# A fused decoder layer on one core: the input norm with its weight spread in PSUM, the first 256 tokens finished ahead

## The chip, the core and the metric

The kernel runs on one core of one Trainium2 chip. Times are device microseconds of a whole execution; the figure that counts is the median of the runs. Profiles come from one profiled execution. The engines are TensorE (PE, with its weight loads PEld), VectorE (DVE, `V` in the code), ScalarE (ACT, `S`), GpSimd (POOL, `G`) and SyncE (SP, `SY`), whose queue issues most loads.

## What is computed

One pre-RMSNorm decoder layer for 512 tokens of width 1024, in float32: norm, one wide input projection, three token mixers side by side (sparse attention, a spatial-gating MLP, an RWKV-7 recurrence), gates, a merge, an output projection, an embedding gate and a final norm. The part that matters here is its beginning:

```
h = x * rsqrt(mean(x*x) + 1e-6) * norm_g
proj = h @ w_in[i]
...
blk = kv[:, idx] + pe[:, None, :]
hid = jax.nn.silu(jnp.einsum('bnlgd,ldh->bngh', blk, w1))
```

The compression branch of the attention takes two 128-column pieces of `proj` (keys and values, kv = 0 and 1) and is the first user of `h`. After it come the RWKV projections (`rs_block`).

## The kernel before

Matrix products run in the rounded type fp32r with a split in two: each operand is a high part (a cast on ACT) and a low part (the difference, on VectorE or POOL), and a product is three matmuls, high by high, high by low, low by high. The normed input is kept transposed as `hH` and `hL` (128 channels x 8 x 512 tokens). `wload` (L66 to L80) does the same for weights: a load of 256 KB on SP's queue into one of four `wr` buffers, the cast L78, the difference L79. `wparts` gathers the pieces; `fm_block` is 24 matmuls of 512 columns for 128 output channels.

The kernel is written with a framework whose planner places the instructions of each engine in an order of its own from a simulated timeline; waits on data and on buffers are put in by it. `tc.issue_after(ins)` makes the instructions in its block that run on the engine of `ins` come after it there.

At the start POOL makes the constants (identity, masks, indicator matrices, L94 to L133), SP loads `x` in four pieces of 128 tokens (L182), and the norm loop (L211 to L226) does for each piece t: the sum of squares on ACT (L214), mean and epsilon on VectorE (L215), the power -1/2 on POOL (L216), the row factor on VectorE over 1024 columns (L217), and then for each half a of the channels four transposes on PE into PSUM (L222), the product with the weight as a per-partition column on VectorE into the buffer `tg` (L224), the cast on ACT into `hH` (L225) and the difference into `hL`, on POOL for a = 0 and on VectorE for a = 1 (L226). The weight column `ngp` comes from a PE transpose of norm_g (L209, L210).

The norm's buffers (pool `xp`) lie on the left side of SBUF; when the pool is closed its place is taken by others, among them `cpp` with `kc2`, `w2t` and `w1t`. The compression weights are loaded, cast and split at L251, held behind a cast of the second 128 tokens on ACT, with the low part on VectorE. Then come the compression products (L252 to L265), in two halves of 256 tokens and for kv = 0 and 1: 24 matmuls of 256 columns each into one of two PSUM buffers `mm_ps`, evicted by four ACT copies into `kc2`. The parameter rows `prow` are loaded by 13 small DMAs (L267), transposed on PE (L269) and copied to `par`, which the RWKV evictions and `blk` (L294) read. `hid` (L301) is the compression's hidden product with `w1t`.

## Time and profile before

| what | value |
|---|---|
| median of 3 runs | 745.41 us (745.38 to 746.82) |
| profiled execution, its own time | 747.35 us |
| its span | 745.6 us |
| PE busy | 716.0 us (96%) |
| VectorE, ACT, POOL busy | 407.6, 354.2, 288.2 us |

The span is what the trace of the core covers; the execution's time has a little around it. An engine's timeline gives for each instruction (or merged group) its start, its duration and, in brackets, how long the engine stood before it and what released it. PE is busy nearly throughout, so its idle stretches are the first thing to look at.

### The profile page before, as it was taken

The numbers are of one execution on the slowest core, as the hardware profiler recorded it, in microseconds if no ns is written. First come the engines' busy times: TensorE is split into PE (matmuls) and PEld (weight loads), VectorE is DVE, ScalarE is ACT, GpSimd is POOL, SyncE is SP. The second block draws the span as 40 slices with busy tenths as digits, with TensorE's granted clock in tenths as the row PEclk, the third lists the DMA queues.
The fourth block names the chain that finished last, engine by engine and source line by source line (L and its number), as shares of the span: only waits on it lengthen the run. The fifth ranks groups of instructions, "written<-read, shape, count | busy, mean of one in ns | idle before, by whom it ended". The sixth has DMA issues, their size and how long they took to land.

```text
span 745.6 us, 13074 instructions
## 1 busy us (share of the span) xinstructions
PE 716.0 (96%) x4941; PEld 606.6 (81%) x4941; DVE 407.6 (55%) x775; ACT 354.2 (48%) x743; POOL 288.2 (39%) x276
## 2 busy tenths in 40 slices
PE   4899999999999999999999999989999999999995
PEld 4788788999878987779877778767877888998995
DVE  6531587758933773645676565397554222226345
ACT  6554555542372332234565554576554333227453
POOL 6444740120220272300144345323445565256563
PEclk9999999999999999999999999999999999999998
DMA  6853122124546364336433212201228333132212
GB/s 200 182 136 100 48 80 71 44 87 140 156 113 215 101 172 124 107 115 203 135 94 105 57 44 70 71 16 42 54 60 267 100 89 124 58 113 72 78 64 114
DMA packets 106689, 78.73 MB, mean 106 GB/s; under 512 B 5569, under 2 KB 97282, under 8 KB 106626
## 3 DMA queue, kind: packets, MB, share of 16 engines
q1 hardware_dynamic: 105890, 75.27, 35.1%
q10 hardware_dynamic: 736, 2.63, 0.9%
q8 instruction: 39, 0.64, 0.4%
q14 instruction: 24, 0.20, 0.1%
HBM read 67.91 MB, written 9.96 MB: 104 GB/s over the span
## 4 chain that ended last, share of the span: by engine, by line
PE 87%; DVE 5%; ACT 2%; issue 2%; DMA 1%; POOL 1%; SPq 1%; ACTq 0%; POOLq 0%; DVEq 0%
PE mm_ps L62 69%; PE s_ps L62 3%; PE o_ps L62 2%; PE g_ps L62 2%; PE p_ps L872 2%; DMA w1t<-in_cmp_w_dram 1%; PE Yp L62 1%; PE r_ps L62 1%; DVE mx L858 1%; PE st_ps L62 1%; PE mx_ps L62 1%; DVE pl L876 1%; PE u_ps L62 1%; PE bk_ps L477 1%; ACT wh L78 1%
## 5 line engine op out<-in xcount | busy, mean ns | idle before, releaser
L79 POOL TENSOR_TENSOR wl<-wr,wh 128x512 fp32r<-128x512 f32 x144 | 192.5, 1345 | 276.5 <-ACT wh L78 255.5
L78 ACT CAST wh<-wr 128x512 fp32r<-128x512 f32 (+1 forms) x194 | 119.4, 620 | 169.6 <-PE mm_ps L62 117.6
L62 PE MATMUL mm_ps<-hH,wh 128*128 128x512 f32 (+1 forms) x440 | 174.2, 396 | 3.8 <-ACT kc L265 2.3
L62 PE MATMUL mm_ps<-hL,wh 128*128 128x512 f32 (+1 forms) x440 | 171.1, 389 | 0.0
L62 PE MATMUL mm_ps<-hH,wl 128*128 128x512 f32 (+1 forms) x440 | 170.7, 388 | 0.4 <-DVE wl L79 0.4
L62 PEld LDWEIGHTS mm_ps<-hH,wh 128*128 128x128 f32 x440 | 82.9, 188 | 21.3 <-ACT kc L265 2.5
L62 PEld LDWEIGHTS mm_ps<-hH,wl 128*128 128x128 f32 x440 | 82.7, 188 | 18.0 <-DVE wl L79 0.6
L62 PEld LDWEIGHTS mm_ps<-hL,wh 128*128 128x128 f32 x440 | 83.0, 189 | 16.5 <-issue 0.2
L62 PE MATMUL mm_ps<-wh,hL 128*128 128x256 f32 (+1 forms) x224 | 64.9, 290 | 0.0
L62 PE MATMUL mm_ps<-wh,hH 128*128 128x256 f32 (+1 forms) x224 | 63.8, 286 | 0.0
L62 PE MATMUL mm_ps<-wl,hH 128*128 128x256 f32 (+1 forms) x224 | 63.6, 285 | 0.0
L79 DVE TENSOR_TENSOR wl<-wr,wh 128x512 fp32r<-128x512 f32 (+1 forms) x50 | 38.0, 769 | 25.2 <-ACT wh L78 25.1
L62 PEld LDWEIGHTS mm_ps<-wh,hL 128*128 128x128 f32 x224 | 42.2, 188 | 1.1 <-issue 0.5
L62 PEld LDWEIGHTS mm_ps<-wh,hH 128*128 128x128 f32 x224 | 42.0, 188 | 1.2 <-issue 0.5
L62 PEld LDWEIGHTS mm_ps<-wl,hH 128*128 128x128 f32 x224 | 42.2, 188 | 0.5
L876 DVE TENSOR_TENSOR pl<-p_ps,ph 128x512 fp32r<-128x512 f32 x40 | 27.2, 685 | 25.9 <-ACT ph L875 25.9
L62 PE MATMUL mm_ps<-ysH,wh 128*128 128x512 f32 x96 | 38.6, 402 | 0.1
L62 PE MATMUL mm_ps<-ysL,wh 128*128 128x512 f32 x96 | 38.4, 400 | 0.2 <-DVE ysL L722 0.2
L62 PE MATMUL mm_ps<-ysH,wl 128*128 128x512 f32 x96 | 38.2, 398 | 0.0
L859 ACT ACTIVATE P<-s_ps,mx 128x512 f32<-128x512 f32 (+3 forms) x64 | 33.4, 532 | 7.9 <-DVE mx L858 5.5
L62 PE MATMUL mm_ps<-wh,mH 128*128 128x256 f32 x128 | 36.1, 286 | 0.6 <-DVE x L921 0.6
L62 PE MATMUL mm_ps<-wl,hT 128*128 128x256 f32 x128 | 35.9, 281 | 0.0
(336 smaller groups left out, 1437.6 us busy)
## 6 DMA issues: line engine op xcount, KB each, us to landing
wr<-in_w_in_dram SPq DMA_DIRECT2D x130, 256.0 KB
wr<-in_w_branch_dram SPq DMA_DIRECT2D x24, 256.0 KB
wr<-in_w_o_dram SPq DMA_DIRECT2D x16, 256.0 KB
wr<-in_w_ple_gate_dram SPq DMA_DIRECT2D x16, 256.0 KB
xs__129<-in_x_dram SPq DMA_DIRECT2D x4, 512.0 KB
w1t<-in_cmp_w_dram SPq DMA_DIRECT2D x4, 512.0 KB
x<-in_x_dram ACTq DMA_DIRECT2D x4, 512.0 KB
out_dram<-x SPq DMA_DIRECT2D x8, 256.0 KB
```

The lines of the kernel that those rows point to most:

```text
L62: return PE.matmul(o, a, b, start=start, stop=stop, **kw).ins
L78: S.copy(h[:, :m], raw[:, :m])
L79: ph_["l"].tensor_tensor(l[:, :m], raw[:, :m], f(h[:, :m]), OP.subtract)
L477: PE.transpose(ps[:, c - c0, :], bk[:, c, 0:2].rearrange("p s t -> p (s t)"), ident)
L858: V.tensor_reduce(mx[:, hh:hh + 1], s_ps[:, :W], axis=AX.X, op=OP.max, negate=True)
L859: S.activation(P[:, hh, :W], s_ps[:, :W], AF.Exp, bias=mx[:, hh:hh + 1], accum_out=sm[:, hh:hh + 1])
L872: PE.transpose(p_ps[:, hh * 128:hh * 128 + 128], P[:, hh, kt * 128:kt * 128 + 128], ident)
L876: V.tensor_tensor(pl, p_ps, f(ph), OP.subtract)
```

## The change

The norm weight is no longer a column applied after the transpose. It is loaded as one row, and two f32 matmuls with a row of ones spread it over all 128 partitions in PSUM (`ngb`); one VectorE operation per half (`x_turn`) then multiplies `x` by the row factor and the spread weight before the transpose. So the transposed PSUM tile is final: ACT casts it into `hH` (`x_hi`), and VectorE takes the difference from it (`x_low`), for all halves. `tg` is gone. The factor (`x_fac`) is wholly on POOL.

The order is written out and pinned on PE, ACT, VectorE and POOL: tokens 0 to 255 go through all steps before the squares of the others. The compression weights are loaded between the pieces of `x`, and cast and split (the low part on POOL) at given places. Matmuls of the identity with itself (`warm`) are put on PE at the start: 3 before the spread, 9 behind it, 1 after each of the first four transposes. In the first half of the compression products the low-weight matmuls come last, and four of the steps are held behind transposes of the later tokens (`XTT`).

POOL makes most constants, and clears `prow`, only after the last of the four weight low parts (`pws[3]`). The pool `xp` lies on SBUF's other side, so that `cpp` doesn't take its place.

```diff
--- before.py
+++ after.py
@@ -18,11 +18,10 @@
 NEG = -1e30
 WE, NR, NH, NL = 560, 4, 5, 5
 NG = 6
-XL = "GV"
-XB = 4
-XP = 3
-KL = "V"
-KCA = 3
+XP = 4
+WU = (3, 9, 1)
+XTT = {(0, 8): (2, 0), (0, 11): (2, 1), (1, 4): (3, 0), (1, 8): (3, 1)}
+KL = "G"
 BS = 3
 BO = 1
 BP = 2
@@ -64,19 +63,29 @@
 
     ph_ = {"l": V}
 
-    def wload(segs, nk):
+    def wraw(segs, nk):
         n = sum(s[2] for s in segs)
         m = nk * n
         raw = wp.tile([128, WE], F32, tag="wr", name="wr", bufs=NR)
-        h = wp.tile([128, WE], R, tag="wh", name="wh", bufs=NH)
-        l = wp.tile([128, WE], R, tag="wl", name="wl", bufs=NL)
         v = raw[:, :m].rearrange("p (k n) -> p k n", n=n)
         o = 0
         for w, c0, cn, k0 in segs:
             SY.dma_start(v[:, :, o:o + cn], w.rearrange("(k p) c -> p k c", p=128)[:, k0:k0 + nk, c0:c0 + cn])
             o += cn
-        S.copy(h[:, :m], raw[:, :m])
-        ph_["l"].tensor_tensor(l[:, :m], raw[:, :m], f(h[:, :m]), OP.subtract)
+        return raw, m, n
+
+    def whi(raw, m, n):
+        h = wp.tile([128, WE], R, tag="wh", name="wh", bufs=NH)
+        return h, S.copy(h[:, :m], raw[:, :m])
+
+    def wlo(raw, m, n, h, eng):
+        l = wp.tile([128, WE], R, tag="wl", name="wl", bufs=NL)
+        return l, eng.tensor_tensor(l[:, :m], raw[:, :m], f(h[:, :m]), OP.subtract)
+
+    def wload(segs, nk):
+        raw, m, n = wraw(segs, nk)
+        h, _ = whi(raw, m, n)
+        l, _ = wlo(raw, m, n, h, ph_["l"])
         return (h[:, :m].rearrange("p (k n) -> p k n", n=n), l[:, :m].rearrange("p (k n) -> p k n", n=n))
 
     def wparts(segs, nk):
@@ -93,47 +102,8 @@
 
     ident = const.tile([128, 128], F32, name="ident")
     make_identity(nc, ident)
-    identb = const.tile([128, 128], BF, name="identb")
...
     mhalf = const.tile([128, 32], F32, name="mhalf")
     G.memset(mhalf, -0.5)
-    bones = const.tile([128, 128], BF, name="bones")
...
-    ng8 = const.tile([8, 128], F32, name="ng8")
-    ngp = const.tile([128, 8], F32, name="ngp")
 
     par = const.tile([128, 128], F32, name="par")
     pcol = {}
@@ -171,19 +141,24 @@
 
 
     hcp = []
+    pw_ctx = ExitStack()
+    pw = pw_ctx.enter_context(tc.tile_pool(name="pw", bufs=1, side="right"))
     xp_ctx = ExitStack()
-    xp = xp_ctx.enter_context(tc.tile_pool(name="xp", bufs=1))
+    xp = xp_ctx.enter_context(tc.tile_pool(name="xp", bufs=1, side="right"))
     xps = xp_ctx.enter_context(tc.tile_pool(name="xps", bufs=XP, space=PSUM))
     xs_ = xp.tile([128, 4, 1024], F32, name="xs_")
     ssx = xp.tile([128, 4], F32, name="ssx")
     rsx = xp.tile([128, 4], F32, name="rsx")
-    S.dma_start(ng8, norm_g[0].rearrange("(a b) -> a b", b=128))
+    ngr = xp.tile([1, 1024], F32, name="ngr")
+    one = xp.tile([1, 128], F32, name="one")
+    S.dma_start(ngr, norm_g)
+    G.memset(one, 1.0)
+    kcr = [[], []]
     for t in range(4):
         SY.dma_start(xs_[:, t, :], x[t * 128:(t + 1) * 128, :])
-    pw_ctx = ExitStack()
-    pw = pw_ctx.enter_context(tc.tile_pool(name="pw", bufs=1, side="right"))
+        if t % 2:
+            kcr[t // 2] = [wraw([(w_in, O_NKC + 128 * (t // 2), 128, k0)], 4) for k0 in (0, 4)]
     prow = pw.tile([128, 128], F32, name="prow")
-    G.memset(prow, 0.0)
     row = 0
     pls = []
     for nm, src in (("mu", rk_mu), ("w0", rk_w0), ("a0", rk_a0),
@@ -205,26 +180,129 @@
     dr = {}
     for nm, w in (("su", 512), ("sv", 512), ("sz", 512), ("rz", 512), ("nz", 512), ("y1", 512), ("sg", 512)):
         dr[nm] = tc.dram_tile([NG * 128 if nm == "sg" else 512, w], F32, name="dr_" + nm)
-    ng_ps = xps.tile([128, 8], F32, tag="par", name="ng_ps", bufs=1)
-    PE.transpose(ng_ps, ng8, ident[0:8, 0:8])
-    V.tensor_copy(ngp, ng_ps)
-    for t in range(4):
-        ts = slice(t * 128, (t + 1) * 128)
+
+    pin = tc.keep_in_program_order
+    wu = pmm.tile([128, 512], F32, tag="mm", name="wu")
+
+    def warm(n):
+        for _ in range(n):
+            pin(PE.matmul(wu[:, 0:128], ident, ident, start=True, stop=True))
+
+    warm(WU[0])
+    ngb = xps.tile([128, 2, 512], F32, tag="ngb", name="ngb", bufs=1)
+    for a in range(2):
+        pin(PE.matmul(ngb[:, a, :], one, ngr[:, a * 512:a * 512 + 512], start=True, stop=True))
+    warm(WU[1])
+    xts, trs = {}, {}
+    kch, kcl = [[None] * 2, [None] * 2], [[None] * 2, [None] * 2]
+
+    def x_sum(t):
         sqj = xp.tile([128, 1024], F32, tag="sqj", name="sqj", bufs=2)
-        S.activation(sqj, xs_[:, t, :], AF.Square, accum_out=ssx[:, t:t + 1])
-        V.tensor_scalar(rsx[:, t:t + 1], ssx[:, t:t + 1], 1.0 / 1024, 1e-6, op0=OP.mult, op1=OP.add)
-        G.tensor_tensor(rsx[:, t:t + 1], rsx[:, t:t + 1], mhalf[:, 0:1], OP.pow)
-        V.tensor_scalar(xs_[:, t, :], xs_[:, t, :], rsx[:, t:t + 1], None, op0=OP.mult)
+        pin(S.activation(sqj, xs_[:, t, :], AF.Square, accum_out=ssx[:, t:t + 1]))
+
+    def x_fac(t):
+        r = rsx[:, t:t + 1]
+        pin(G.tensor_scalar(r, ssx[:, t:t + 1], 1.0 / 1024, 1e-6, op0=OP.mult, op1=OP.add))
+        pin(G.tensor_tensor(r, r, mhalf[:, 0:1], OP.pow))
+
+    def x_turn(t, w):
         for a in range(2):
-            ks = slice(4 * a, 4 * a + 4)
+            xa = xs_[:, t, a * 512:a * 512 + 512]
+            pin(V.scalar_tensor_tensor(xa, xa, rsx[:, t:t + 1], ngb[:, a, :], op0=OP.mult, op1=OP.mult))
             ps = xps.tile([128, 4, 128], F32, tag="xt", name="xt_ps")
             for k in range(4):
-                PE.transpose(ps[:, k, :], xs_[:, t, (4 * a + k) * 128:(4 * a + k + 1) * 128], ident)
-            tg = xp.tile([128, 4, 128], F32, tag="tg", name="tg", bufs=XB)
-            V.tensor_tensor(tg, ps, ngp[:, 4 * a:4 * a + 4].unsqueeze(2).to_broadcast([128, 4, 128]), OP.mult)
-            hcp.append(S.copy(hH[:, ks, ts], tg).ins)
-            (V if XL[a] == "V" else G).tensor_tensor(hL[:, ks, ts], tg, f(hH[:, ks, ts]), OP.subtract)
+                q = PE.transpose(ps[:, k, :], xa[:, k * 128:k * 128 + 128], ident)
+                if w:
+                    pin(q)
+            xts[t, a] = ps
+            trs[t, a] = q.ins
+            warm(w)
+
+    def x_hi(t, a):
+        ts = slice(t * 128, (t + 1) * 128)
+        hcp.append(pin(S.copy(hH[:, 4 * a:4 * a + 4, ts], xts[t, a])).ins)
+
+    def x_low(t):
+        ts = slice(t * 128, (t + 1) * 128)
+        for a in range(2):
+            h = slice(4 * a, 4 * a + 4)
+            pin(V.tensor_tensor(hL[:, h, ts], xts[t, a], f(hH[:, h, ts]), OP.subtract))
+
+    def k_hi(kv, i):
+        kch[kv][i], q = whi(*kcr[kv][i])
+        pin(q)
+
+    def k_lo(kv, i):
+        kcl[kv][i], q = wlo(*kcr[kv][i], kch[kv][i], G)
+        pws.append(pin(q).ins)
+
+    pws = []
+    for t in range(2):
+        x_sum(t)
+        x_fac(t)
+        x_turn(t, WU[2])
+    k_hi(0, 0)
+    k_lo(0, 0)
+    x_hi(0, 0)
+    x_hi(0, 1)
+    k_hi(0, 1)
+    k_lo(0, 1)
+    x_low(0)
+    x_hi(1, 0)
+    x_hi(1, 1)
+    x_low(1)
+    for t in range(2, 4):
+        x_sum(t)
+        x_fac(t)
+        x_turn(t, 0)
+    for i in range(2):
+        k_hi(1, i)
+        k_lo(1, i)
+    for t in range(2, 4):
+        x_hi(t, 0)
+        x_hi(t, 1)
+        x_low(t)
     xp_ctx.close()
+
+
+    with tc.issue_after(pws[3]):
+        identb = const.tile([128, 128], BF, name="identb")
+        V.tensor_copy(identb, ident)
...
+        G.memset(prow, 0.0)
 
 
     AR = keep.tile([128, 2, 4, 512], F32, name="AR")
@@ -238,26 +316,33 @@
     kcst = const.tile([128, 2, 2, 32], R, name="kcst")
     vcst = const.tile([128, 2, 128], R, name="vcst")
     hm = const.tile([128, 4], F32, name="hm")
-    G.memset(hm, 0.0)
-    for hh in range(4):
-        G.memset(hm[32 * hh:32 * hh + 32, hh:hh + 1], 1.0)
+    with tc.issue_after(pws[3]):
+        G.memset(hm, 0.0)
+        for hh in range(4):
+            G.memset(hm[32 * hh:32 * hh + 32, hh:hh + 1], 1.0)
     cp_ctx = ExitStack()
     cpp = cp_ctx.enter_context(tc.tile_pool(name="cpp", bufs=1))
     cps = cp_ctx.enter_context(tc.tile_pool(name="cps", bufs=1, space=PSUM))
     kc2 = cpp.tile([128, 2, 2, 512], F32, name="kc2")
 
     G.memset(kc2[64:128, :, :, 496:512], 0.0)
-    with tc.issue_after(hcp[KCA]):
-        wkc = [wparts([(w_in, O_NKC + 128 * kv, 128)], 8) for kv in range(2)]
+    wkc = [[[w[i][:, c:c + 128] for i in range(2) for c in range(0, 512, 128)] for w in (kch[kv], kcl[kv])]
+           for kv in range(2)]
     for half in range(2):
         c0 = half * 256
         for kv in range(2):
             hs, ls = wkc[kv]
             ps = pmm.tile([128, 512], F32, tag="mm", name="mm_ps")
-            for k in range(8):
-                mm(ps[:, :256], hs[k], hH[:, k, c0:c0 + 256], k == 0, False)
-                mm(ps[:, :256], hs[k], hL[:, k, c0:c0 + 256], False, False)
-                mm(ps[:, :256], ls[k], hH[:, k, c0:c0 + 256], False, k == 7)
+            for k in range(12):
+                with ExitStack() as tie:
+                    if half == 0 and (kv, k) in XTT:
+                        tie.enter_context(tc.issue_after(trs[XTT[kv, k]]))
+                    if k < 8:
+                        mm(ps[:, :256], hs[k], hH[:, k, c0:c0 + 256], k == 0, False)
+                        mm(ps[:, :256], hs[k], hL[:, k, c0:c0 + 256], False, False)
+                    else:
+                        for j in (2 * k - 16, 2 * k - 15):
+                            mm(ps[:, :256], ls[j], hH[:, j, c0:c0 + 256], False, j == 7)
             sh = 16 if half else 0
             with tc.issue_after(hcp[-1]):
                 for g in range(2):
```

## Rows read from the trace of the kernel before

**Rows 1.** The page's first part: busy us, share of span, instructions.

```profile
PE 716.0 (96%) x4941; PEld 606.6 (81%) x4941; DVE 407.6 (55%) x775; ACT 354.2 (48%) x743; POOL 288.2 (39%) x276
```

**Rows 2.** Table by stretches of 10 us: busy us and instructions, granted clock, DMA.

```profile
0.00:10.00 10.00, 1.89 (x9) 1.82 (x10) 3.15 (x10) 5.86 (x9) 6.72 (x43) 1.00 0.82 284
10.00:20.00 10.00, 8.17 (x51) 7.19 (x50) 10.00 (x16) 6.24 (x12) 6.83 (x6) 1.00 0.45 125
20.00:30.00 10.00, 7.66 (x65) 7.45 (x63) 4.59 (x11) 6.16 (x15) 4.54 (x7) 1.00 0.57 142
30.00:40.00 10.00, 9.51 (x59) 7.43 (x59) 4.52 (x2) 3.00 (x8) 2.88 (x2) 1.00 1.23 237
```

**Rows 3.** PE's waits, first 60 us: total, times, longest, in us.

```profile
PE ng_ps L209 <- DMA ng<-in_norm_g_dram: 3.1, 1, 3.1
PE mm_ps L62 <- ACT kc L265: 2.3, 1, 2.3
...
PE hid L62 <- DMA w1t<-in_cmp_w_dram: 0.5, 1, 0.5
```

**Rows 4.** POOL timeline, first 80 us: start, us, operation, idle before, releaser.

```profile
0.93 0.20 POOL L99 MEMSET trib<- 128x128 bf16 x1
...
6.37 0.49 POOL L243 MEMSET hm<- 32x1 f32 x4
6.95 0.56 POOL L216 TENSOR_TENSOR rsx<-rsx,mhalf 128x1 f32<-128x1 f32 x1
```

**Rows 5.** Groups by shape, POOL, then PE: busy us, mean ns, idle before.

```profile
L79 POOL TENSOR_TENSOR wl<-wr,wh 128x512 fp32r<-128x512 f32 x144 | 192.5, 1345 | 276.5 <-ACT wh L78 255.5 <-issue 9.7 <-DMA x<-in_x_dram 4.1
...
L935 POOL TENSOR_SCALAR s<-s 128x1 f32<-128x1 f32 x4 | 0.9, 231 | 0.3
...
L62 PE MATMUL bo<-m,bor 128*128 128x512 f32 x8 | 4.1, 592 | 0.0
```

**Rows 6.** ACT timeline, first 60 us.

```profile
4.50 1.06 ACT L214 ACTIVATE sqj<-xs__129 128x1024 f32<-128x1024 f32 x1 [1.80 <-DMA xs__129<-in_x_dram]
...
14.55 2.18 ACT L78 CAST wh<-wr 128x512 fp32r<-128x512 f32 x4
...
20.59 0.62 ACT L78 CAST wh<-wr 128x512 fp32r<-128x512 f32 x1 [1.35 <-DMA wr<-in_w_in_dram]
...
23.85 0.36 ACT L264 COPY kc<-mm_ps 64x256 f32<-64x256 f32 x1 [2.12 <-DVE hL L226]
```

**Rows 7.** VectorE timeline, first 70 us.

```profile
7.55 0.75 DVE L217 TENSOR_SCALAR xs__129<-xs__129,rsx 128x1024 f32<-128x1024 f32 x1 [1.71 <-POOL rsx L216]
...
9.76 1.29 DVE L224 TENSOR_TENSOR tg<-xt_ps,ngp 128x512 f32<-128x512 f32 x2
...
21.31 2.43 DVE L226 TENSOR_TENSOR hL<-tg,hH 128x512 fp32r<-128x512 f32 x2
```

**Rows 8.** Timeline of PE's weight loads, 8 to 24 us.

```profile
8.35 3.28 PEld L222 LDWEIGHTS xt_ps<-ident,xs__129 128*128 128x128 f32 x16 [5.09 <-DVE xs__129 L217]
11.83 1.57 PEld L222 LDWEIGHTS xt_ps<-ident,xs__129 128*128 128x128 f32 x8 [0.20 <-issue]
...
15.70 0.86 PEld L222 LDWEIGHTS xt_ps<-ident,xs__129 128*128 128x128 f32 x8 [0.19 <-issue]
```

**Rows 9.** PE timeline, first 60 us.

```profile
25.38 0.39 PE L62 MATMUL mm_ps<-hH,wh 128*128 128x256 f32 x1 [2.35 <-ACT kc L265]
...
31.18 0.39 PE L62 MATMUL mm_ps<-hH,wh 128*128 128x512 f32 x1
```

**Rows 10.** SP timeline, first 70 us: DMA issues.

```profile
6.57 2.15 SPq L267 DMA_DIRECT2D prow<-in_rk_mu_dram  x1
...
12.93 1.70 SPq L267 DMA_DIRECT2D prow<-in_cmp_pe_dram  x4
...
17.41 4.38 SPq L76 DMA_DIRECT2D wr<-in_w_in_dram  x4
23.90 2.05 SPq L286 DMA_DIRECT2D w2t<-in_cmp_w_dram  x4
```

More of the change, by code (lines that the diff above doesn't have):

```diff
@@ new lines, in hybrid_kernel @@
+    for t in range(2, 4):
+        x_hi(t, 0)
+        x_hi(t, 1)
+        x_low(t)
+    xp_ctx.close()
+    with tc.issue_after(pws[3]):
+        identb = const.tile([128, 128], BF, name="identb")
+        V.tensor_copy(identb, ident)
+        trib = const.tile([128, 128], BF, name="trib")
+        G.memset(trib, 0.0)
+        G.affine_select(out=trib, in_=trib, pattern=[[-1, 128]], compare_op=OP.is_ge, fill=NEG, base=0,
+                        channel_multiplier=1)
+        cmask = const.tile([128, 4, 32], BF, name="cmask")
+        G.memset(cmask, 0.0)
+        G.affine_select(out=cmask, in_=cmask, pattern=[[128, 4], [-16, 32]], compare_op=OP.is_ge, fill=NEG,
+                        base=-31, channel_multiplier=1)
+        rowm = const.tile([128, 1], F32, name="rowm")
+        G.memset(rowm, 1.0)
+        G.affine_select(out=rowm, in_=rowm, pattern=[[0, 1]], compare_op=OP.is_ge, fill=0.0, base=-31,
+                        channel_multiplier=1)
+        gmask = const.tile([128, 2, 64], BF, name="gmask")
+        G.memset(gmask, 1.0)
+        for r in (0, 64):
+            for ar in range(2):
+                G.affine_select(out=gmask[r:r + 64, ar, :], in_=gmask[r:r + 64, ar, :], pattern=[[1, 64]],
+                                compare_op=OP.is_ge, fill=0.0, base=ar - 1, channel_multiplier=-1)
+        smask = const.tile([128, 8, 64], BF, name="smask")
+        G.memset(smask, 1.0)
+        G.memset(smask[:, :, 0:1], 0.0)
+        tri = const.tile([128, 128], BF, name="tri")
+        G.memset(tri, 1.0)
+        G.affine_select(out=tri, in_=tri, pattern=[[1, 128]], compare_op=OP.is_ge, fill=0.0, base=0,
+                        channel_multiplier=-1)
+        bones = const.tile([128, 128], BF, name="bones")
+        G.memset(bones, 0.0)
+        G.memset(bones[0:64, 0:64], 1.0)
+        G.memset(bones[64:128, 64:128], 1.0)
+        hind = const.tile([128, 4, 8], F32, name="hind")
+        G.memset(hind, 0.0)
+        for q in range(4):
+            for e in range(2):
+                G.memset(hind[e * 64:e * 64 + 64, q, 2 * q + e:2 * q + e + 1], 1.0)
+        G.memset(prow, 0.0)
```

34 lines of the change are left out of this document (removed).

## The prediction

> **What bounds the kernel now.** I read the page's busy shares first. TensorE (PE) is busy for 716.0 us of a span of 745.6 [rows 1], so at most 29.6 us can be had without taking work from it. The table by stretches says where that idle time lies: 8.1 us in the first ten, 1.8 in the next ten, 2.3 in the third, 0.5 in the fourth, 12.8 in all [rows 2]; afterwards PE is full for a long time. The change touches only this start. The list of PE's waits gives each gap its cause [rows 3]: 3.1 us for norm_g, 2.3 for the kc copies on ACT and 0.5 for the w1t load; between the first and the second PE's weight loads stand 5.1 for the first normalized x, until 8.35 [rows 8]. The timelines then show what stands behind each. The POOL timeline: the first pow (L216) starts only at 6.95, because POOL works off constants until 6.86 [rows 4], though ACT began to square the first 128 tokens at 4.50 [rows 6] and was done about 1.15 later. The ACT timeline: the first kc copy starts at 23.85, after 2.12 us of waiting for the last low part hL on VectorE [rows 6]; kc2 lies where the norm's buffers lay, so it waits for their last reader. PE therefore stands from 23.03 to 25.38, then runs the second half of the two compression products without a gap to 31.18 [rows 9]: 48 matmuls in 5.80, 0.121 each. From there on PE is the bound. **The question is how much earlier than 31.18 this point comes.**
>
> **The first transpose.** The square starts at 4.50 as before and ends at 5.65. The factor is now two POOL operations: 0.23 for the small product [rows 5] and 0.57 for pow [rows 4]; with hops it is there at 6.55 instead of 7.52. The product with factor and spread weight takes one PSUM operand; the nearest row, the product that it replaces, took 0.65 for 512 columns [rows 7]. I take 0.7: first half at 7.3, second at 8.0, the next 128 tokens at 8.7 and 9.4. This price speaks against the change: the row-factor product out of SBUF did 1024 columns in 0.75 [rows 7], so the first half is no faster than the whole was, and the second comes 0.65 later. The Trainium skill (VectorE: DVE Perf Modes, Why PSUM operands drop a tier) says why: a PSUM operand takes fp32 out of the faster mode. Were the old 0.375 per half kept, the sum below would be the same, since PE, not VectorE, is late there.
>
> PE's new work comes ahead of the transposes. An f32 matmul is two MATMULs (the bonus product shows 8 for 4 calls [rows 5]). Transposes of 128 columns follow each other at 0.205 and 0.196 at first (16 in 3.28, 8 in 1.57) and at 0.107 after that (8 in 0.86) [rows 8], the ratio of the two clock levels, 1.2 and 2.4 GHz, although the granted clock reads 1.00 in each of these stretches [rows 2]. So the old start has 24 transposes at the lower level before the clock rises. In the new kernel PE can start when ident is there, which I put at 1.5. Three warm matmuls at the lower level (2 x 0.21 each) end at 2.8; the spread weight waits for norm_g until 3.1 [rows 3] and then needs 4 MATMULs of 512 columns: 3.4 at the lower level (16 spacings of 0.21), 1.7 at the upper. The nine warm matmuls behind it take 3.8 or 1.9. They end at 10.4 if PE stays at the lower level through all of it and at 6.8 if it is at the upper from 3.1 on. These are the bounds for a stretch that the trace doesn't show. I take 9.0, nearer to the lower, because the old PE worked through 24 transposes before its clock rose. So the transposes wait for the warm matmuls and not for their data (7.3). The Trainium skill (TensorE: Matmul & The Clock Gate, What's actually happening) says that the throttled state is the default and activity lifts it; the two spacings agree. By that rule the warm matmuls bring the rise forward and the end lies between the two bounds, as I take it; were the clock deaf to them, it would be 10.4.
>
> **The first 256 tokens.** From 9.0 on I take the upper level: four groups of transposes (0.43 each) with a warm matmul (0.21) between end at 11.4. ACT's casts take 0.55 in a row [rows 6]; the fourth ends at 12.15. The low parts are now all on VectorE from PSUM, at the 0.65 to 0.7 of the product from PSUM rather than the last two's 1.2 [rows 7]; that of the third group ends at 12.25. There the compression product of kv=0 starts: 16 matmuls to 14.2. The third 128 tokens come next: square 12.2 to 13.35 on ACT (it now stands behind four casts), factor 14.25, product 15.0, so PE waits 0.85 and transposes at 15.05. Its x load isn't late: 2.1 MB end with it, 7.4 us at the mean 284 GB/s of the first ten [rows 2]. From 15.05 PE has 32 remaining matmuls (3.9) and four transposes (1.7): first half over at 20.65, against 23.03. The last transposes end at 19.7, their cast at 20.45, the four copies of kv=0 (0.37 each [rows 6]) at 21.95; no buffer below them holds them now. The second half starts at 22.0 instead of 25.38 and ends at 27.8 instead of 31.18: **3.4 us**.
>
> **Loads and constants.** w2t and w1t no longer wait for the norm's buffers (before: w2t issued at 23.90, behind the last hL [rows 10]). They can go right after the compression weights, so PE's wait of 0.5 goes too. **Sum 3.9.** The four low parts of the compression weights cost POOL 4 x 1.35 [rows 5]; the last ends near 18.0. Behind it stand the constants, which took POOL from 0.93 to 6.86 [rows 4], some 5.6 us without the parts that stay early: to 23.6. I cost them at nothing, since only prow is wanted early (par, for the first RWKV block's eviction, 5.6 us after 27.8); with that cover gone it is the slow rival. The 13 prow loads were issued from 6.57 to 14.63 [rows 10] with some waiting in it, so they can end near 31 even at that pace, and PE then needs par at 33.4. How the planner's order of what follows may move no row shows; I take zero, and for either side twice the one small wait that this stretch has now (0.5 [rows 3]), a microsecond.
>
> **Against the profiled execution.** It took 747.35 with a span of 745.6, while the median of the runs is 745.41. 3.9 off the span is 741.7, off the execution 743.45, off the median **741.5**.
>
> **Rivals.** (1) The clock rises late or not before the first 256 tokens are through: the nine warm matmuls end at 10.4, transposes cost 0.85 and warm matmuls 0.43, so the four groups end at 15.1 instead of 11.4; 3.7 of the 3.9 are gone, and with a rise half-way 1.5 to 2. Time 743.2 to 745.2. For it: the 24 slow transposes of the old trace; against it: PE works here from 3.1 on without a gap, and the old one's rise came after such work [rows 8]. (2) The gain is given back later: the planner's order changes, RWKV weights come late behind the 2 MB of w1t (at the 142 to 237 GB/s of those stretches [rows 2] 9 to 15 us, so up to 26 if they start when the 3.1 MB of x and compression weights are through, 11 at 284; a further load and cast then lie on the edge of 27.8). Up to 3 us, 744.5. Against it: PE is the bound for most of the rest. (3) Slower: the 13 prow loads stand in SP's queue ahead of the RWKV weights. prow is cleared at 23.6, the loads need some 5.5 without their old waits, 29.1; the first weight load then lands 3.2 after its issue (17.41 to 20.59 [rows 6, 10]) and is cast in 0.6, so PE starts that block at 32.9 instead of 31.18: 1.7 slower, **747.1**. It decides from a clearing of prow at 22 on, and only if the order on SP is so; against it, two weight buffers come free by 13, long before prow does. (4) All goes well: the clock is up before the nine warm matmuls, so that they end near 7.7: a good microsecond more, 740.3, and 739.3 with the microsecond of the order on the good side.
>
> **How the numbers follow.** Forecast (740.3 to 742.8) 0.55, rival 4's better end 0.10, rival 1 0.15, rival 2 0.10, rival 3 0.10. About 0.2% (1.5 us) is what a measurement of this kernel can tell from no change. Faster, below 743.9: the forecast, rival 4 and over half of rival 1, 0.75. Within: the rest of rival 1, rival 2, 0.15. Slower: rival 3, 0.10. The range 739.3 to 745.2 leaves out rival 3 and a part of rival 4, some 0.15 to 0.2.
>
> **What would show it.** Right: first pow near 6.0, first transposes of x at 7.3 to 9.5 and at 0.107 each, second half of the compression products starting near 22, the first 512-column matmul of the RWKV block near 27.8, no wait for w1t. Wrong: x transposes at 0.205 (rival 1); a PE wait for a weight cast or par between 26 and 45 (rivals 2, 3); the start as told but the end not 3.9 earlier, which is then to be sought in the order of the later stages.

## The result, and the profile after

The changed kernel takes **752.99 us** (median of 6, 752.21 to 753.44) against 746.76 for the kernel before, run beside it (745.38 to 748.38): ratio 1.0077, 95% interval 1.0060 to 1.0094. It is slower by some 6 us, where 3.9 us faster was forecast and the range ended at 745.2. The profiled execution took 752.29, its span is 750.6, 5.0 more than before.

The first part of the page of the changed kernel answers [rows 1]: TensorE is busy 10.0 us longer for the same products (the warm matmuls and the spread come on top).

```profile
PE 726.0 (97%) x4976; PEld 614.7 (82%) x4976; DVE 403.0 (54%) x766; ACT 353.6 (47%) x743; POOL 288.3 (38%) x281
```

The table by stretches of 10 us of the changed kernel (as [rows 2]):

```profile
0.00:10.00 10.00, 8.18 (x23) 5.42 (x24) 2.83 (x5) 4.20 (x6) 3.79 (x14) 1.00 0.83 290
...
20.00:30.00 10.00, 5.68 (x42) 5.48 (x42) 3.38 (x6) 4.83 (x12) 6.37 (x31) 0.82 0.78 155
30.00:40.00 10.00, 10.00 (x58) 9.27 (x58) 0.00 (x0) 6.04 (x13) 5.66 (x9) 0.84 0.52 131
```

In the first ten microseconds PE's idle time is filled, but with warm matmuls and the spread. From 20 to 30 us it is idle for 4.3 us, against 2.3 before, and here and in the next ten the granted clock (0.82 and 0.84) falls, which it did not before (1.00). PE's timeline of the changed kernel, to be read beside [rows 9] (L189 warm matmuls, L214 transposes, L61 products):

```profile
7.10 4.21 PE L189 MATMUL wu<-ident 128*128 128x128 f32 x18
11.10 1.06 PE L214 MATMUL xt_ps<-ident,xs__89 128*128 128x128 f32 x4
12.38 0.76 PE L214 MATMUL xt_ps<-ident,xs__89 128*128 128x128 f32 x4
...
22.59 1.18 PE L61 MATMUL mm_ps<-hH,wl 128*128 128x256 f32 x8
28.09 0.58 PE L61 MATMUL mm_ps<-hH,wh 128*128 128x256 f32 x1 [4.32 <-ACT kc L350]
...
36.12 0.39 PE L61 MATMUL mm_ps<-hH,wh 128*128 128x512 f32 x1
```

The first half of the compression products ends at 23.77 (before 23.03), PE then stands 4.32 us (before 2.35), and the second half takes 8.03 us, from 28.09 to 36.12 (before 5.80). The three differences, 0.74, 1.97 and 2.23, are the 4.94 by which the first RWKV matmul is late (36.12 against 31.18), and the span is 5.0 longer: all of the loss lies before 36 us. ACT's timeline of the changed kernel, beside [rows 6], says why PE stood (L79 casts of weights, L223 casts of the transposes, L349 kc copies):

```profile
24.61 0.62 ACT L79 CAST wh<-wr 128x512 fp32r<-128x512 f32 x1 [5.25 <-DMA wr<-in_w_in_dram]
25.13 1.55 ACT L223 CAST hH<-xt_ps 128x512 fp32r<-128x512 f32 x3
26.56 0.37 ACT L349 COPY kc<-mm_ps 64x256 f32<-64x256 f32 x1
```

The cast at 24.61 belongs to the first RWKV block, which PE needs only after the second half. It stood in ACT's queue waiting for its load, and behind it three casts of `hH`, whose last transposes had started at 22.2, and all the kc copies. The load was late because of what stands ahead of it in SP's queue; the issues in the changed kernel, and then a line of the kernel before that belongs to [rows 10]:

```profile
8.73 6.37 SPq L376 DMA_DIRECT2D w1t<-in_cmp_w_dram  x4
15.22 7.13 SPq L73 DMA_DIRECT2D wr<-in_w_in_dram  x4
```
```profile
25.99 5.92 SPq L291 DMA_DIRECT2D w1t<-in_cmp_w_dram  x4
```

w1t, which before waited for the norm's buffers, is now issued ahead of the RWKV weights. The first of these loads is even issued earlier than before (15.22 against 17.41), but it is cast 9.4 us after its issue and not 3.2 [rows 6, 10]. Finally, the clock after the pause, in stretches of 2.5 us (changed kernel; the granted clock is the last column but two):

```profile
27.50:30.00 2.50, 1.91 (x9) 1.91 (x10) 1.10 (x3) 1.96 (x6) 1.94 (x15) 0.50 0.03 7
30.00:32.50 2.50, 2.50 (x13) 2.50 (x13) 0.00 (x0) 1.17 (x2) 0.37 (x4) 0.50 0.15 22
32.50:35.00 2.50, 2.50 (x21) 2.50 (x20) 0.00 (x0) 1.54 (x5) 2.04 (x2) 0.87 0.32 90
```

It is at its lower level (0.50, 1.2 GHz) from 27.5 to 32.5 us: thirteen matmuls in 2.5 us there, against twenty-one later. So the second half paid for the pause a second time.

### The profile page after: what moved, and what is told of

Read it like the earlier page. It is cut to its first block, busy times and chain, and to the rows that moved or that the text cites. A ratio compares the mean times of both kernels' runs of the same rounds, so it can differ in the third digit from the quotient of the medians.

```text
span 750.6 us, 13138 instructions
## 1 busy us (share of the span) xinstructions
PE 726.0 (97%) x4976; PEld 614.7 (82%) x4976; DVE 403.0 (54%) x766; ACT 353.6 (47%) x743; POOL 288.3 (38%) x281
## 4 chain that ended last, share of the span: by engine, by line
PE 87%; DMA 4%; DVE 4%; ACT 2%; issue 1%; SPq 0%; POOL 0%; ACTq 0%; POOLq 0%; DVEq 0%
PE mm_ps L61 69%; PE s_ps L61 3%; PE o_ps L61 2%; PE g_ps L61 2%; PE p_ps L957 2%; DMA wr<-in_w_in_dram 1%; PE Yp L61 1%; DMA zs<-dr_nz 1%; DMA xs__89<-in_x_dram 1%; DMA w1t<-in_cmp_w_dram 1%; DMA pt<-in_p_dram 1%; PE u_ps L61 1%; PE r_ps L61 1%; DVE mx L943 1%; PE st_ps L61 1%
## 5 line engine op out<-in xcount | busy, mean ns | idle before, releaser
L83 POOL TENSOR_TENSOR wl<-wr,wh 128x512 fp32r<-128x512 f32 x148 | 197.8, 1345 | 284.7 <-ACT wh L79 261.0
L79 ACT CAST wh<-wr 128x512 fp32r<-128x512 f32 (+1 forms) x194 | 119.3, 620 | 169.0 <-PE mm_ps L61 118.4
L61 PE MATMUL mm_ps<-hH,wh 128*128 128x512 f32 (+1 forms) x440 | 174.0, 397 | 4.5 <-ACT kc L350 4.3
L61 PE MATMUL mm_ps<-hL,wh 128*128 128x512 f32 (+1 forms) x440 | 171.3, 391 | 0.3 <-DVE hL L229 0.3
L61 PE MATMUL mm_ps<-hH,wl 128*128 128x512 f32 (+1 forms) x440 | 167.1, 390 | 0.0
L61 PEld LDWEIGHTS mm_ps<-hH,wh 128*128 128x128 f32 x440 | 84.1, 191 | 22.0 <-ACT kc L350 4.5
L61 PEld LDWEIGHTS mm_ps<-hL,wh 128*128 128x128 f32 x440 | 84.2, 191 | 16.5 <-DVE hL L229 0.5
L61 PEld LDWEIGHTS mm_ps<-hH,wl 128*128 128x128 f32 x440 | 81.6, 191 | 16.8
L61 PE MATMUL mm_ps<-wh,hL 128*128 128x256 f32 (+1 forms) x224 | 64.0, 286 | 0.0
L61 PE MATMUL mm_ps<-wh,hH 128*128 128x256 f32 (+1 forms) x224 | 63.9, 288 | 0.0
L61 PE MATMUL mm_ps<-wl,hH 128*128 128x256 f32 (+1 forms) x224 | 63.7, 285 | 0.0
L83 DVE TENSOR_TENSOR wl<-wr,wh 128x512 fp32r<-128x512 f32 (+1 forms) x46 | 33.3, 731 | 23.1 <-ACT wh L79 22.9
L61 PEld LDWEIGHTS mm_ps<-wl,hH 128*128 128x128 f32 x224 | 42.3, 189 | 0.8 <-issue 0.2
L61 PEld LDWEIGHTS mm_ps<-wh,hH 128*128 128x128 f32 x224 | 41.9, 188 | 1.2 <-issue 0.5
L61 PEld LDWEIGHTS mm_ps<-wh,hL 128*128 128x128 f32 x224 | 42.2, 188 | 0.7 <-issue 0.2
L61 PE MATMUL mm_ps<-ysH,wh 128*128 128x512 f32 x96 | 38.5, 402 | 0.3 <-ACT ysH L806 0.3
L61 PE MATMUL mm_ps<-ysL,wh 128*128 128x512 f32 x96 | 38.4, 400 | 0.2 <-DVE ysL L807 0.2
L61 PE MATMUL mm_ps<-ysH,wl 128*128 128x512 f32 x96 | 38.2, 397 | 0.0
L61 PE MATMUL mm_ps<-wh,mH 128*128 128x256 f32 x128 | 36.1, 286 | 0.6 <-DVE x L1006 0.6
L61 PE MATMUL mm_ps<-wl,mH 128*128 128x256 f32 x128 | 35.8, 281 | 0.0
```

The source lines that it names most:

```text
L61: return PE.matmul(o, a, b, start=start, stop=stop, **kw).ins
L79: return h, S.copy(h[:, :m], raw[:, :m])
L83: return l, eng.tensor_tensor(l[:, :m], raw[:, :m], f(h[:, :m]), OP.subtract)
```

## The experiments

**The cast behind the last hH cast.** The changed kernel, with the first RWKV block's ACT work ordered behind ACT's last cast of `hH`:

```diff
     for b in (12, 4, 5, 6, 7):
-        rs_block(b)
+        with ExitStack() as es:
+            if b == 12:
+                es.enter_context(tc.issue_after(hcp[-1]))
+            rs_block(b)
```

> The changed kernel with one edit: all ScalarE instructions of the first RWKV block (its two weight casts and its eviction) are held behind the last cast of the norm's high parts. Loads stay as they are, so the block's weights still land at about 24.6. Theory A (a cast that waits for a late load stands in ACT's queue ahead of three casts of hH, and the PE pause that follows lowers its clock): no 5.2 us wait on ACT ahead of the hH casts, the second half of the compression products starts near 24.8 instead of 28.1, runs at the upper clock level (5.8 instead of 8.0 us) and ends near 30.6 instead of 36.1; span near 745.2, 5.4 below the changed kernel's 750.6. Rival B (the late load itself costs, wherever the cast stands): PE waits instead at the first RWKV block for its weights, span 749 or more. Rival C (the slow second half has another cause than the pause): it still takes 8.0 us, span near 747.5.

Measured: 747.61 us, ratio to the kernel before 0.9996 (0.9981 to 1.0011). PE's and ACT's timelines of this run:

```profile
25.02 0.38 PE L61 MATMUL mm_ps<-hH,wh 128*128 128x256 f32 x1 [1.10 <-ACT kc L350]
30.73 0.39 PE L61 MATMUL mm_ps<-hH,wh 128*128 128x512 f32 x1
```
```profile
23.01 0.59 ACT L223 CAST hH<-xt_ps 128x512 fp32r<-128x512 f32 x1 [0.80 <-PE xt_ps L214]
23.49 0.37 ACT L349 COPY kc<-mm_ps 64x256 f32<-64x256 f32 x1
...
25.00 0.62 ACT L79 CAST wh<-wr 128x512 fp32r<-128x512 f32 x1
```

The load is as late as before, but nobody stands behind it: the pause is 1.10, the second half takes 5.71 at the upper level, and 5.4 us of PE's start are back. That one place in ACT's queue is the cause of the slowdown is shown. That the forecast gain then appears is not: 0.45 us at the first RWKV matmul, which is less than the interval of the time can tell from nothing.

**w1t behind the first block's weights.** The four w1t loads issued after the first two RWKV weight loads; ACT's order left to the planner:

```diff
+    pre12, dq = [], []
+    for k0 in (0, 4):
+        pre12.append(wraw([(w_in, O_RS + 128 * 12, 128, k0)], 4))
+        dq.append(wq[0].ins)
...
+          with tc.issue_after(dq[-1]):
             SY.dma_start(w1t[lh * 64:lh * 64 + 64], ...)
```

> The changed kernel with one edit: the four w1t loads (2 MB) are issued behind the two weight loads of the first RWKV block on SP's queue instead of ahead of them. Theory A: the block's first load, issued near 9 to 12, lands before 18, no cast waits for a load ahead of the hH casts, the second half of the compression products starts near 24.8 and ends near 30.6; w1t lands by 30; span near 745, like the run that only holds the cast. Rival B (w1t late costs as much at the hidden product): a PE wait of 1 us or more for w1t, span 747 or more.

Measured: 750.83 us, ratio 1.0036 (1.0022 to 1.0050), a miss. The second half did start at 24.80; then ACT and PE show:

```profile
31.83 0.62 ACT L81 CAST wh<-wr 128x512 fp32r<-128x512 f32 x1 [4.93 <-DMA wr<-in_w_in_dram]
```
```profile
34.03 0.79 PE L61 MATMUL mm_ps<-hH,wh 128*128 128x512 f32 x1 [3.35 <-ACT kc L360]
34.62 0.63 PE L61 MATMUL mm_ps<-hL,wh 128*128 128x512 f32 x1
35.05 0.63 PE L61 MATMUL mm_ps<-hH,wl 128*128 128x512 f32 x1
```

The same thing happens one load further on: the cast of the second RWKV block, whose load is now the one behind w1t, stands ahead of the second half's copies; PE stops for 3.35 us and comes back with 0.43 between 512-column matmuls instead of 0.23. Moving a load only moves the victim while ACT's order stays.

**The side alone, both ways.** The changed kernel with `xp` on the left again (`side="right"` taken out of one line), and the kernel before with only `xp` on the right (`pw`, which lies on that side too, is opened ahead of it):

```diff
...
-    xp = xp_ctx.enter_context(tc.tile_pool(name="xp", bufs=1))
+    xp = xp_ctx.enter_context(tc.tile_pool(name="xp", bufs=1, side="right"))
```

> The changed kernel with one edit: the norm's pool lies on the left side of SBUF again, so kc2, w2t and w1t take its place and wait for its last reader. Theory A: w2t and w1t come late as before the change, the first RWKV block's loads are early, no 5.2 us wait on ACT; the first kc copy waits for the last low part (near 24.1), the second half starts near 25.6 at the upper clock level and ends near 31.4; span near 746, 4.7 below the changed kernel. If w1t, now behind the 13 prow loads, comes late, 1 to 3 us are lost at the hidden product (747 to 749). Rival (the side has nothing to do with it): span near 750.6.

> The kernel before with one part of the change alone: the norm's pool on the right side of SBUF. Theory A: the kc copies no longer wait for the last low part of hL, the pause of 2.35 us ahead of the second half shrinks to 0.5, and the first RWKV block's loads, now behind w1t on SP's queue, land near 28, where they cost 0 to 1.5 us; span 743.5 to 745.5 against 745.6. Rival (the side alone is what makes it slow): 748 or more.

Left again: 750.60 us, ratio 1.0042 (1.0023 to 1.0060). The start is good, PE at 24.42 and 30.21, a microsecond ahead of before. But now w1t, which waits for the norm's buffers again, comes late, as the expectation had allowed for (0.5 us of waiting before [rows 3], 1.02 here), the first `iv_ps` is at 207.34 where it was at 206.47, and in the profiled execution the clock fell there, behind waits in the recurrence:

```profile
43.19 3.68 PE L61 MATMUL hid<-w1t,blk 128*64 128x128 f32 x62 [1.02 <-DMA w1t<-in_cmp_w_dram]
```
```profile
206.00:224.00 18.00, 16.58 (x307) 13.36 (x306) 7.66 (x8) 12.69 (x19) 4.17 (x3) 0.81 0.28 87
```

(before: 1.00 in this stretch.) So a part of the loss comes ahead of the dip, and that the dip makes up the rest in all of its runs is an inference from one execution. Right in the kernel before: 750.97 us, ratio 1.0042 (1.0028 to 1.0057); ACT and PE:

```profile
30.56 0.62 ACT L78 CAST wh<-wr 128x512 fp32r<-128x512 f32 x1 [4.60 <-DMA wr<-in_w_in_dram]
```
```profile
33.76 0.63 PE L62 MATMUL mm_ps<-hH,wh 128*128 128x512 f32 x1 [3.62 <-ACT kc L265]
```

So the move of the buffers alone, without any of the norm's new code, sets the trap: freed from the wait for the norm's buffers, w1t goes ahead of RWKV weights. In the kernel before, the wait that the change removes (PE 2.3 us, [rows 3]) had also kept 2 MB out of the way.

**Fewer warm matmuls.** e1_hold with `WU = (3, 0, 1)` instead of `(3, 9, 1)`, and with `(0, 0, 0)`:

> The run that holds the cast, without the nine warm matmuls behind the spread of the weight (3 ahead of it and 1 after each early group of transposes stay). Theory A (x is ready at 8.1, and the nine warm matmuls, all at the lower clock level, hold the first transposes back to 10.9): first transposes at 8.1, all four early groups at the lower level (0.85 each), the fourth done near 12.8 instead of 14.5, second half of the compression products starting 1.7 earlier than with them (23.3 against 25.0), time 1.5 to 2 below the run that holds the cast. Rival B (the clock then rises later): the first half of the compression products runs at 0.21 a matmul instead of 0.12 for a part of its 48; for all of it that would be 4.5 us, and the second half would start at 25 or later; no gain or a loss of up to 3 us.

> The run that holds the cast, with no warm matmul at all. Theory A: first transposes at 8.1, four groups of 0.85 without a matmul between, the fourth done near 11.5, second half starting near 22.0; time 2.5 to 3 below the run that holds the cast, if the clock rises before the first compression product near 12.5. Rival B (without them the clock rises later): parts of the 48 matmuls of the first half at 0.21 instead of 0.12, up to 4.5 us lost, second half at 24 to 26.

Measured: 747.45 us (ratio 0.9996, 0.9979 to 1.0013) and 747.94 (1.0014, 0.9999 to 1.0028). PE in the first, then PE and ACT in the second:

```profile
12.16 0.73 PE L214 MATMUL xt_ps<-ident,xs__89 128*128 128x128 f32 x4
...
23.14 0.39 PE L61 MATMUL mm_ps<-hH,wh 128*128 128x256 f32 x1 [1.11 <-ACT kc L350]
...
27.30 0.39 PE L61 MATMUL mm_ps<-hH,wh 128*128 128x256 f32 x1 [1.06 <-ACT kc L350]
30.26 0.50 PE L61 MATMUL mm_ps<-hH,wh 128*128 128x512 f32 x1
```
```profile
7.94 3.67 PE L214 MATMUL xt_ps<-ident,xs__89 128*128 128x128 f32 x16 [1.02 <-DVE xs__89 L211]
...
21.86 0.39 PE L61 MATMUL mm_ps<-hH,wh 128*128 128x256 f32 x1 [1.11 <-ACT kc L350]
...
27.43 0.39 PE L61 MATMUL mm_ps<-hH,wh 128*128 128x256 f32 x1 [2.48 <-ACT kc L350]
30.39 0.48 PE L61 MATMUL mm_ps<-hH,wh 128*128 128x512 f32 x1
```
```profile
25.27 0.62 ACT L79 CAST wh<-wr 128x512 fp32r<-128x512 f32 x1 [3.46 <-DMA wr<-in_w_in_dram]
```

Without the nine the second half starts at 23.14, without any warm matmul at 21.86, 1.9 and 3.2 us before e1_hold. So at the start they cost more than they gave: PE ran at the lower level until 12.2 to 12.7 in all three kernels (the groups of four at 12.38 in the changed kernel and 12.16 in e5_no9 are the first to go faster). The moment itself moves from execution to execution: with the same eighteen MATMULs ahead, the first faster group starts at 11.02 in f4_fill and only behind 12.38 in f2_hold_pair (both below). But the gain stops at the same door: the RWKV weights land near 25 us whatever PE did, the cast waits ahead of kc copies again, now in the middle of the second half (PE waits 1.06 and 2.48 us), and the first RWKV matmul moves by 0.3 to 0.5.

**All of it together.** e1_hold, w1t behind the loads of the first two RWKV blocks, `prow` cleared at the start, and no nine:

> The changed kernel with four edits together: the first RWKV block held behind the last hH cast, w1t issued behind the weight loads of the first two RWKV blocks, prow cleared at the start (so that its 13 loads go ahead of them), and no nine warm matmuls. Theory A: as the run without the nine (second half near 23.3), no wait of a cast for a load before 35, par read before 30, no PE wait for w1t (landed by 36, hidden product at 38 or later); time within 0.5 of the run without the nine, since PE was not waiting for these loads there. Rival (late loads and par cost more than the list of waits shows): 1.5 us or more below it.

747.34 us, ratio 0.9992 (0.9975 to 1.0009). Here the start works: PE at 23.17, first RWKV matmul at 29.07, 2.1 us ahead of before. 2.1 us would be a ratio of 0.9972, outside the interval. Where it went: PE waits 0.85 us between that matmul and the first `iv_ps`, 0.65 of it ahead of 46.12 us, where the kernel before waits 0.49 (for w1t). From 84 to 206 us PE has next to no idle time in either (0.2 in e10_all), yet the 128 Gram matmuls (`g_ps`), counted from each one's start to the next instruction's, took 16.1 us (15.5 in e1_hold, 14.7 before), and the last of them and the first `iv_ps` behind them are only 0.2 and 0.4 ahead. Before, then e10_all:

```profile
99.41 1.17 PE L62 MATMUL g_ps<-AR,bk 64*128 64x128 f32 x16
...
159.88 1.16 PE L62 MATMUL g_ps<-AR,bk 64*128 64x128 f32 x8
...
206.47 2.21 PE L62 MATMUL iv_ps<-itmp,Gt 32*32 32x32 f32 x128
```
```profile
159.67 1.16 PE L61 MATMUL g_ps<-AR,bk 64*128 64x128 f32 x8
...
206.04 2.21 PE L61 MATMUL iv_ps<-itmp,Gt 32*32 32x32 f32 x128
```

**The Gram matmuls in alternating order.** In the kernel before a run of sixteen of them, which by the program read both partition halves, takes 1.17 us and a run of eight from one half 1.16. So a theory was at hand: the earlier start changes how often two from different halves meet. The 128 matmuls pinned in the program's order, in the kernel before, in e1_hold and in e10_all:

```diff
-                    mm(gps[e][:, c - c0], st, AR[r0:r0 + 64, :, q, cs], True, True)
+                    tc.keep_in_program_order(PE.matmul(gps[e][:, c - c0], st, AR[r0:r0 + 64, :, q, cs],
+                                                       start=True, stop=True))
```

> Kernel before, one edit: the 128 Gram matmuls (g_ps) are pinned in the order in which the program writes them, so that the one that reads partitions 0 to 63 and the one that reads 64 to 127 always alternate. In the trace of before a run of sixteen of them (both halves alternating) took 1.10 us, 0.069 us each, and a run of eight from one half 1.09 us, 0.136 each; together they took 14.7 us, in e1_hold 15.5 and in e10_all 16.1, and TensorE has no idle time between 85 and 206 us in any of the three. Theory G (what e10 had won by 40 us is given back there, because its Gram matmuls meet in pairs less often): here all 128 take about 8.8 us, the first iv_ps matmul starts about 5.9 us earlier than 206.5, at about 201, and the whole kernel takes about 740 us. Rival D (from 85 us on VectorE sets the pace, 17 to 18 of each 20 us busy, and TensorE's order only moves its waits): TensorE shows idle time at g_ps, iv_ps stays within 1 us of 206.5, and the time within 1.5 us of the kernel before.

> e1_hold with the Gram matmuls pinned in alternating order as in f1_before_pair. Theory G: the gain that e1_hold has at the first RWKV matmul (30.73 against 31.18) and the 6.7 us of its Gram matmuls both stay: first iv_ps at about 200.5, about 0.5 us ahead of f1_before_pair, time about 739 to 740. Rival D: iv_ps where it was in e1_hold (206.1), time 745 to 747.5.

> e10_all with the Gram matmuls pinned in alternating order. e10_all reached its first RWKV matmul 2.1 us before the kernel before, and stood only 0.4 us ahead at 206 us. Theory G: with the Gram matmuls at one price in both, first iv_ps comes 1.5 to 2 us ahead of f1_before_pair, at about 199, and the time is about 738. Rival D: iv_ps within 0.5 us of f1_before_pair, wherever that lies, because the chain of VectorE decides, and no difference between the two times.

Measured: 750.81 (ratio 1.0037, 1.0023 to 1.0052), 747.18 (0.9992, 0.9977 to 1.0006) and 746.12 us (0.9986, 0.9964 to 1.0008). The Gram matmuls took 11.6 us in the first, 3 less (not the 8.8 of the forecast, since two mostly went ahead alone); all the same its first `iv_ps` came at 209.28 and not near 201, and the time rose. The rival, that VectorE's pace would show as PE waits at `g_ps`, isn't seen either. But neither `iv_ps` nor the time judges the theory here. The stretch from the first RWKV matmul to the first `iv_ps` (with a few instructions at its edges) before, in e10_all and in f1_before_pair, PE first:

```profile
31.18:206.47 175.29, 174.79 (x1125) 149.00 (x1123) 113.04 (x182) 81.41 (x162) 54.88 (x46) 1.00 0.38 101
```
```profile
29.07:206.04 176.97, 176.12 (x1125) 149.56 (x1123) 114.67 (x182) 81.42 (x161) 55.14 (x46) 1.00 0.39 100
```
```profile
31.11:209.28 178.17, 177.47 (x1147) 150.15 (x1146) 113.60 (x182) 83.46 (x165) 57.47 (x48) 1.00 0.40 104
```

In f1_before_pair 22 matmuls more, of the block products, stand ahead of `iv_ps`: the edit moved other work too. Behind it PE waits 6.1 us from 206 to 335 us, 2.4 before, and the granted clock from 206 to 330 is 0.94, 0.99 before. So the run has more waits and a lower clock to pay, and its time doesn't refute the theory. Before and e10_all, though, have the same 1125 there, and e10_all takes 1.7 us longer for them: 1.4 of it are the Gram matmuls, most of the rest waits. And they do meet less often: of the 128, 19 start within 20 ns of the one ahead before (14.7 us in all), 13 in e1_hold (15.5), 11 in e10_all (16.1) and 50 in f1_before_pair (11.6). So by this count, in one execution of each, most of what e10_all had won is gone in Gram matmuls that go ahead alone, and the 0.4 us left are too few for the time to show. **No run restores the old pairing and leaves the rest of the order as it is, so this is counted and not shown by an experiment**; f3_all_pair, with the pairs and the good start, has the lowest ratio of all, but not one that is told apart from 1.

**Matmuls in the pause.** The changed kernel with 40 and then, mended, 21 matmuls of the identity between the two halves, the second half behind them (the lines are those of the mended one):

```diff
+    fl = xps.tile([128, 2, 512], F32, tag="ngb", name="fl", bufs=1)
+    with tc.issue_after(last):
+        for _ in range(FILL):
+            fq = PE.matmul(fl[:, 0, 0:128], ident, ident, start=True, stop=True).ins
```

> The changed kernel with 40 matmuls more (identity on identity, 128 columns, into a tile of their own that nobody reads) between the two halves of the compressed K and V projection, where TensorE stood for 4.32 us, and the second half behind them. Nothing else is changed, so that the late cast and the late copies stay. Theory C (the second half took 8.03 us and not 5.8 because the granted clock had fallen to its lower level in the pause, 0.50 between 27.5 and 32.5 us): the fill lasts some 4 us, the second half starts at about 28.1 as before and ends 5.7 to 5.9 us later, the first RWKV matmul starts at about 33.9 and not 36.1, and the time is about 2.2 us below that of the changed kernel, about 750.5. Rival (the second half is slow because its own weights or PSUM buffers come late, or because SBUF is shared with the transfers): it takes 8 us again, and the time stays at about 752.5.

> As f4_fill, mended. There the fill waited for the last low part of the transposes, whose PSUM space it had been given, and started at 30.15 instead of 23.7; 11 us later the second half took 5.75 us. Here 21 such matmuls write the space of the spread norm weight, which has been free since 10 us, and the first half's matmuls stand ahead of them in the program; all else as in the changed kernel, the late cast included. Theory C (the lower clock after the pause is worth 2.2 us of its own): the fill lasts from 23.8 to about 28, the second half starts at 28.1 to 28.3, takes 5.7 to 5.9 us, the first RWKV matmul starts at about 34.0 and not 36.1, the time is about 750.5 against 752.5 of the changed kernel. Rival: the clock falls all the same, 8 us, 752.5. In both a time well above that of the kernel before (747.5) remains, because the late copies are left as they are.

With 40: 763.03 us, ratio 1.0201 (1.0178 to 1.0225). The fill's PSUM space was that of the last transposes, so it waited for their low part:

```profile
30.15 11.41 PE L358 MATMUL fl<-ident 128*128 128x128 f32 x80 [7.18 <-DVE hL L229]
41.31 0.37 PE L61 MATMUL mm_ps<-hH,wh 128*128 128x256 f32 x1
...
47.06 0.48 PE L61 MATMUL mm_ps<-hH,wh 128*128 128x512 f32 x1
```

A fault of the experiment, of the kind that it was to study; still, the second half took 5.75 us, as at the upper level, behind a fill that had kept PE busy for 11 us. With 21, in space that is free: 751.54 us, ratio 1.0051 (1.0028 to 1.0074).

```profile
23.26 4.85 PE L286 MATMUL fl<-ident 128*128 128x128 f32 x42
28.71 0.39 PE L62 MATMUL mm_ps<-hH,wh 128*128 128x256 f32 x1 [0.60 <-ACT kc L368]
...
34.47 0.48 PE L62 MATMUL mm_ps<-hH,wh 128*128 128x512 f32 x1
```

The copies are 0.6 later here, and all the same the first RWKV matmul is 1.65 earlier: the second half takes 5.76 instead of 8.03. So some 2.2 us of the loss are the clock's, shown at this place; in the time, 752.99 and 751.54 are not told apart by their intervals.

## Why the prediction was wrong, step by step

- **The factor and the products: the prices right, the start not.** The factor's pow ran from 5.61 to 6.17 (forecast: there at 6.55), and four products took 2.72, 0.68 each (0.7). But the first half was to be ready at 7.3, and its product only started at 7.40: it needs the spread, which PE had done at about 7.1 (in e6_nowarm, where it starts at 7.13, the profile names `ngb` as what it waited for). The chain of the forecast has no wait for the spread. It cost nothing here, as the transposes stood behind the warm matmuls until 11.1; without the nine PE waits 1.02 us for the product (e5_no9, first transposes at 8.26). The w1t wait of 0.5 [rows 3] was gone. `prow` was cleared at 22.0 (forecast 23.6), from which the slower rival would have decided, but its loads were issued from 22.4, behind the RWKV weights: that rival's order didn't occur.
- **The nine warm matmuls, mis-sized.** The end was put at 9.0, bounds 6.8 to 10.4 (their terms add up to 6.7 and 10.3); it was 11.1, outside both. The spread started at 3.4, not 3.1, and took 3.7, and the eighteen MATMULs took 0.22 each, the lower level throughout, and the first group of transposes after them 1.28 up to the next. So the first rival held for the most part: the transposes of 256 tokens were through at 14.3, not 11.4. The argument that PE works from 3.1 on without a gap, and the clock therefore rises earlier, failed: it rose at 12.2 to 12.7 with that work, without the nine and without any (e6_nowarm), and from 11.0 to some 13 between executions of one start. The Trainium skill (TensorE: Matmul & The Clock Gate, What's actually happening) says that activity lifts the throttle; that it lifts it sooner here, as the prediction read it, the runs don't bear out. In e1_hold, where nothing else went wrong, the second half started at 25.02 against the forecast 22.0: these 3.0 us are that step's price.
- **The last casts of hH at 20.45 and the copies at 21.95: the step that failed.** It took ACT's work as ready when its data was. The second rival had the late load, behind w1t's 2 MB (these through by 26 at the latest, the cast on the edge of 27.8; measured 24.61), but asked only whether the RWKV block itself would wait, at 27.8. It didn't name what is queued on ACT behind the cast that waits. That cost 3.07 us (28.09 against e1_hold's 25.02). The Trainium skill (TensorE: Matmul & The Clock Gate, Architectural detail: the array is 16× 32×32, not 1× 128×128) states that ACT's queue is strictly first in, first out; the row with 5.25 us of waiting and three ready casts behind it agrees.
- **The second half's 5.8 us (22.0 to 27.8), wrong by 2.23.** The price of a matmul was carried over from a stretch at the upper clock; the pause ahead of it took the clock away. No rival had a clock that falls again.
- **The sum.** Forecast at the first RWKV matmul 3.4 earlier, measured 4.94 later: 8.3 us apart, of which 3.0 + 3.07 + 2.2.
- **"From there on PE is the bound", right for the waits, too coarse for the time.** From 84 to 206 us PE had no idle time, before and after. The loss came through whole (4.94 at 36 us, 5.0 in the span, 6 in the medians). The gain of e10_all did not: 1.7 of its 2.1 us were gone at the first `iv_ps`, 1.4 of them in Gram matmuls that cost more in another order. A full PE says that nothing waits, not that the same matmuls take the same time.

## What to carry to other kernels

When a change frees a buffer, follow the loads that this lets go early, and then the instruction that waits for each load that they overtake: on an in-order engine it holds up everything behind it, needed or not. Pin or tie the order of such a cast together with the change that moves its load. Behind an early start, compare the price of the same instructions too, and not only the waits. And before adding work to warm a clock, look in a trace at whether the clock rises sooner for it.

## What the runs showed of the hardware

- The granted-clock column reads 1.00 in the first 20 us, while the spacing of transposes and warm matmuls is that of the lower level until 12.38 us in the changed kernel (0.22 a MATMUL against 0.11 later) and until 11.02 in f4_fill; so at the start the spacing has to be read.
- After PE pauses of 1.1 us (e1_hold and others) the clock stayed up, nor did it fall after those of 2.35 (before, [rows 9]) and 2.48 (e6_nowarm). After pauses of 3.35, 3.62, 4.32 and 7.18 us PE came back at the lower level. But the length alone doesn't decide it: after one of 1.61 us the granted clock of e4_bright was 0.66 from 16 to 21 us, and after one of 2.13 us that of f1_before_pair 0.57 from 15 to 19, where the kernel before, after 1.41, has 1.00. In the recurrence an idle time of about 1.7 us, in two pieces, was followed by a fall in the kernel before and by none in e1_hold:

```profile
318.00:322.00 4.00, 2.33 (x30) 1.72 (x27) 2.67 (x6) 1.36 (x3) 0.00 (x0) 0.95 0.48 153
322.00:326.00 4.00, 3.94 (x46) 2.93 (x45) 0.17 (x1) 1.54 (x3) 0.00 (x0) 0.62 0.34 129
```
```profile
318.00:322.00 4.00, 2.32 (x31) 1.62 (x31) 2.21 (x6) 1.30 (x3) 0.00 (x0) 1.00 0.57 183
322.00:326.00 4.00, 3.94 (x60) 3.12 (x57) 1.36 (x5) 2.19 (x5) 0.00 (x0) 1.00 0.41 145
```

- Executions of one kernel differ in this: of the runs of the kernel before that stand beside e1_hold, those with a mean granted clock of 0.993 took 745.3 to 747.1 us, those with 0.988 748.1 to 748.9.
- Matmuls over 64 partitions, taken from both halves in turn, run two at a time: sixteen in 1.17 us, eight from one half in 1.16; fourteen pinned in turn (f1_before_pair, at 161.25) take 1.16, of which the first and the last go alone. The Trainium skill (TensorEngine Tiling (Array Packing), Theoretical Speedup) gives up to twice the rate for such a contraction; these rows agree.
